# A two-layer diffusion backbone on one core: layer 0's gate stage with TensorE in the program's order, column sums two steps behind their squares, one adaLN row block for each gate tile

## The chip, the cores and the metric

The kernel runs on one core of one Trainium2 chip. The metric is the device time of one execution in microseconds (us), taken as the median of several runs; lower is better.

The engines are named as in the profile: PE is TensorE (matrix products into PSUM), PEld its weight loads, DVE is VectorE, ACT is ScalarE, POOL is GpSimd, SP is SyncE, which issues most DMAs. Each engine works through its own instruction stream in order and waits on semaphores for the others.

## The reference, cut to what matters

Two post-norm layers over 1024 latent tokens with 256 context tokens ahead of them share one weight set per layer: layer 0 is multi-head latent attention, layer 1 differential attention. All of it is float32.

```
m = silu(c) @ ada_w[i] + ada_b[i]            # adaLN: shift, scale, gate, for c and for c_ctx
h = x * (1 + scale) + shift                   # and h_c from ctx in the same way
q_lat, kv_lat, k_pe, gate = split(h @ w_in)   # 256 + 128 + 32 + 1024 columns
q = rms_norm(q_lat, g_qa) @ w_qb              # 16 heads of 64 + 32
kv = rms_norm(kv_lat, g_kva) @ w_kvb          # 16 heads of 64 + 64
k_pe, q_pe = rope(k_pe), rope(q_pe)
o = softmax(q k^T * scale) v
x = layer_norm(ALPHA * x + gate_ada * ((o * silu(gate)) @ out_w), ln_g, ln_b)
```

The stage at issue is the one that computes `silu(gate)` for all 1280 tokens. Beside it the kernel prepares the up-projection weights of layer 0 and does the adaLN sums that are needed later: shift and scale of layer 1 and the gate of layer 0.

## The kernel before, in words

Matrix products are done in pieces: every float32 operand is split into a high and a low part, and `mm3` (L185 to L187) issues three matmuls for each product. The first stretch computes h and its split, then the latent columns of `w_in` for ten tiles of 128 tokens (`lat_post` transposes the result and writes the rope keys to the DRAM buffer `kp_d`).

The gate stage (`p0g`) then runs over four column blocks q of 256 columns and ten token tiles each. One `gate_tile` is 24 matmuls of 128x256 into a PSUM bank of tag `a` or `d`, two of each, a SiLU on ACT (tile `gg`) and a DMA to `sg_d`. `gate_w` loads and splits the next block's weights: eight loads `wgs`, a cast on ACT (`wgH`) and a subtraction on POOL (`wgL`). The two weight buffers take turns, so block q+2 can be split only when block q has been used.

Beside the tiles runs the generator `beside_gates`, from which two steps are taken for each tile. It has two parts:

- `up_weights` loads `w_qb` in four pieces of 128x768 and the key half of `w_kv` in two of 128x512, scales each on DVE, casts it on ACT and forms the low part on POOL; applies rope to the keys in three chunks of tokens (`kr`); and bounds the column norms of the V, K and Q weights. For that ACT squares 512 columns into `wsq`, PE sums the columns with a matrix of ones (`onr`) into a bank of tag `c`, of which there are two, and DVE takes the maximum into `vm` (L415). With the largest rope key, broadcast by one matmul (L438), these give the power-of-two scales `vsc0`, `ksc0`, `qsc0`. Last it writes the split rope keys to `kpf_d`.
- `ada_dve` goes through three thirds of `ada_w`: shift and scale of layer 1, gate of layer 0. For each of eight row blocks of 512 KB (`adw`, three buffers) DVE adds it, times one scalar per row, into two accumulators (L467, L469), one for c and one for c_ctx, one buffer each. At the end of a third PE sums over partitions: 8 matmuls of one column per accumulator for shift and scale (L476), 4 matmuls of 512 columns for the gate (L488).

After the stage `ab1_of` and `h1_range` bound layer 1's input (two matmuls, L507, and some twenty small DVE instructions), and layer 0's first head follows: `prod_k`, `prod_q` and `prod_v0` with three PSUM pairs of tag `a`.

What sets the order: most of the program is issued in the order of a scheduler that works at build time with its own estimates, engine by engine. In a `manual_schedule` block PE instead keeps the order in which the program issues its instructions; `man.close()` ends such a block. Before, PE is under the scheduler from the end of the latent products to the end of the gate stage. The instruction streams are fixed at build time either way.

Of the kernel before, what the change touches and what calls it, by code (L numbers as in the profile page):

```python
# [9 lines left out]
F32 = mybir.dt.float32  # L10
# [43 lines left out]
def hybrid_kernel(  # L54
# [317 lines left out]
    def up_weights(pa):  # L372

        for j in range(2):
            for hh in range(2):
                c = slice(hh * 768, hh * 768 + 768)
                ws = pa.tile([P, 768], F32, tag="ws2", bufs=1, name=nm("ws2"))
                sp.dma_start(ws, w_qb[j * P:(j + 1) * P, c])
                dve.tensor_scalar_mul(ws, ws, gqa[:, j:j + 1])
                split(wqH[:, j, c], wqL[:, j, c], ws, e_lo=pool)  # L380
                yield
        for hh in range(2):
            c = slice(hh * 512, hh * 512 + 512)
            kv_weight(c, wkH[:, c], wkL[:, c], rot(pa, [P, 512], F32, "wkv"))
            yield

        kr = pa.tile([ROPE, NTOK], F32, name="kr")
        for c0, n in CHUNKS:
            c = slice(c0, c0 + n)
            kt = pa.tile([ROPE, 512], F32, tag="kt", name=nm("kt"))  # L390
            sp.dma_start(kt[:, :n], kp_d[:, c])
            if c0 < SEQ:
                tabs = []
                for j in range(2):
                    tb = pa.tile([ROPE, 512], F32, tag=f"ktab{j}", name=nm("ktab"))
                    sp.dma_start(tb, cs0[j, :ROPE, c])
                    tabs.append(tb)
                rope(kt, n, tabs[0], tabs[1], rot(pa, [ROPE, 512], F32, "rsw"), kr[:, c])
            else:
                dve.tensor_copy(kr[:, c], kt[:, :n])  # L400
            yield


        vm = pa.tile([P, 8], F32, name="vm")

        def col_norms(dst, parts, n):
            wsq = pa.tile([P, 2, 512], F32R, tag="wsq", name=nm("wsq"))
            for c0 in range(0, n, 512):
                for j, f in enumerate(parts):
                    f(wsq[:, j, :], slice(c0, c0 + 512))  # L410
                yield
                bk = bank("c")
                for j, f in enumerate(parts):
                    pe.matmul(bk, onr, wsq[:, j, :], start=j == 0, stop=j == len(parts) - 1)
                dve.tensor_reduce(vm[:, 6:7], bk, axis=AX.X, op=ALU.max)  # L415
                if c0:
                    dve.tensor_tensor(dst, dst, vm[:, 6:7], op=ALU.max)
                else:
                    dve.tensor_copy(dst, vm[:, 6:7])
                yield  # L420

        def sq_v(dst, c):
            wv = pa.tile([P, 512], F32, tag="wvq", bufs=1, name=nm("wvq"))
            sp.dma_start(wv, w_kv[:, 1024 + c.start:1024 + c.stop])
            act.activation(dst, wv, AF.Square, scale=gkva)

        yield from col_norms(vm[:, 0:1], [sq_v], 1024)
        yield from col_norms(vm[:, 1:2], [lambda d_, c: act.activation(d_, fv(wkH[:, c]), AF.Square)], 1024)
        yield from col_norms(vm[:, 2:3], [lambda d_, c, j=j: act.activation(d_, fv(wqH[:, j, c]), AF.Square)
                                          for j in range(2)], 1536)  # L430
# [4 lines left out]
        dve.tensor_reduce(vm[:ROPE, 3:4], kr, axis=AX.X, op=ALU.max, apply_absolute_value=True)  # L435
# [11 lines left out]
        kh_ = pa.tile([P, 768], F32, tag="ws2", bufs=1, name=nm("ws2")).bitcast(F16)[:ROPE, :NTOK]  # L447
        kl_ = pa.tile([P, 2, 512], F32R, tag="wsq", name=nm("wsq")).rearrange(
            "p a b -> p (a b)").bitcast(F16)[:ROPE, :NTOK]
# [5 lines left out]
    man.close()  # L455

    def ada_dve(tile_, bk_, thirds):

        for layer, g in thirds:
            acc = [tile_(f"acc{s}") for s in range(2)]  # L460
            for k in range(KT):
                w = tile_("adw")
                sp.dma_start(w, ada_w[layer, k * P:(k + 1) * P, g * D:(g + 1) * D])
                for s, a_ in enumerate(acc):
                    ck = sc[:, 2 * k + s:2 * k + s + 1]
                    if k == 0:
                        dve.tensor_scalar_mul(a_, w, ck)  # L467
                    else:
                        dve.scalar_tensor_tensor(a_, w, ck, a_, op0=ALU.mult, op1=ALU.add)  # L469
                yield  # L470
            yield
            if g < 2:
                cb = bk_()
# [8 lines left out]
                continue  # L482
            gr = tile_("adw")[:1, :]
            sp.dma_start(gr, ada_b[layer:layer + 1, g * D:(g + 1) * D])
            for s, a_ in enumerate(acc):
                for c0 in (0, 512):
                    bk = bk_()
# [3 lines left out]
                yield  # L491

# [7 lines left out]
    def h1_range(bk):  # L500

        for i in range(2):
            dve.tensor_reduce(hm[:, i:i + 1], ab1[:, i, :, :].rearrange("p a b -> p (a b)"), axis=AX.X, op=ALU.max,
                              apply_absolute_value=True)
# [975 lines left out]
```

## Time and profile before

| | us |
|---|---|
| median of 3 runs | 1860.38 |
| the runs | 1852.12, 1860.38, 1868.84 |
| span of the profiled execution | 1870.0 |
| gate stage, first tile behind the latent products to the last | 99.7 to 250.0 |
| first score of layer 0 | 284.2 |

The profiled execution is given by its span, from the first to the last instruction; it lies 1.2 us above the slowest of the runs shown, and no time of its own is listed beside it. In the profile, "idle" is the time in which an engine had nothing to run, and the name behind the arrow is the instruction whose end let it go on. A matmul's row shows its latency; neighbouring matmuls overlap, so the time of a tile is read from start to start. The granted clock is the share of full TensorE speed in a stretch.

### The profile page before, as it was taken

How to read it: one execution, taken by the hardware profiler on the slowest of the kernel's cores; microseconds unless marked ns; L12 is line 12 of the kernel's file. 1: busy time of each engine (PE TensorE's matmuls, PEld its weight loads, DVE VectorE, ACT ScalarE, POOL GpSimd, SP SyncE). 2: the span in 40 equal slices, each digit the busy share in tenths (PEclk: the TensorE clock that was granted, in tenths of full speed). 3: DMA queues.
4: the chain of work that ended last, by engine and by line, in shares of the span. 5: the costliest groups of instructions: out<-in, count | busy, mean ns of one | idle time of the engine just before them, and what ended most of it. 6: DMA issues, size and time to landing. Idle time of an engine off the chain costs nothing. (4 is left out here: it accounts for less than half of the span.)

```text
span 1870.0 us, 36547 instructions
## 1 busy us (share of the span) xinstructions
PE 1696.2 (91%) x14468; PEld 1237.0 (66%) x14468; DVE 1245.6 (67%) x2072; ACT 1077.1 (58%) x2143; POOL 835.2 (45%) x741
## 2 busy tenths in 40 slices
PE   7889998999999998868979999999999999988998
PEld 3888965656666565556756576767666666666776
DVE  7546766565565657526764777787877777878674
ACT  3432047867777787711123667676767676767542
POOL 1443026767767676646662213222222222433654
PEclk9999799999999999979999999999999999999999
DMA  8245630111111113043333222222121212224341
GB/s 307 62 126 182 189 108 18 39 33 36 42 44 32 32 41 100 25 164 123 124 127 106 71 63 66 62 64 58 56 49 44 59 46 61 63 53 139 99 131 68
DMA packets 111225, 154.84 MB, mean 83 GB/s; under 512 B 13415, under 2 KB 84679, under 8 KB 111054
## 3 DMA queue, kind: packets, MB, share of 16 engines
q1 hardware_dynamic: 104238, 146.22, 26.1%
q10 hardware_dynamic: 6816, 6.29, 1.0%
q8 instruction: 114, 1.87, 0.4%
q14 instruction: 57, 0.47, 0.1%
HBM read 98.65 MB, written 27.07 MB: 67 GB/s over the span
## 5 line engine op out<-in xcount | busy, mean ns | idle before, releaser
L716 POOL TENSOR_TENSOR pl<-p,ph 128x1024 f16<-128x1024 f32 (+1 forms) x176 | 362.8, 2066 | 155.9 <-ACT ph L715 129.5
L1167 ACT ACTIVATE p<-ps_b,mx 128x512 f32<-128x512 f32 (+1 forms) x384 | 230.6, 618 | 83.1 <-DVE mx L1163 82.7
L696 DVE TENSOR_REDUCE mx<-ps_a 128x1 f32<-128x1024 f32 x128 | 155.6, 1223 | 138.2 <-PE ps_a L694 138.2
L714 ACT ACTIVATE p<-ps_a,esc 128x1024 f32<-128x1024 f32 (+1 forms) x176 | 189.2, 1075 | 100.4 <-PE ps_a L772 94.5
L715 ACT CAST ph<-p 128x1024 f16<-128x1024 f32 (+1 forms) x176 | 177.1, 1006 | 5.5
L1161 DVE TENSOR_REDUCE mx<-ps_b 128x1 f32<-128x512 f32 x256 | 165.6, 682 | 0.0
L785 PE MATMUL ps_d<-Vh,pl 128*128 128x65 f16 x1344 | 147.5, 195 | 5.2 <-POOL pl L716 5.1
L782 PE MATMUL ps_d<-Vh,ph 128*128 128x65 f16 x1344 | 149.5, 196 | 0.0
L784 PE MATMUL ps_d<-Vl,ph 128*128 128x64 f16 x1344 | 148.3, 193 | 0.0
L185 PE MATMUL ps_b<-h1H,wH 128*128 128x512 f16 (+1 forms) x384 | 133.5, 348 | 14.1 <-DVE pl L182 6.7
L185 PE MATMUL ps_b<-wH,h1H 128*128 128x256 f16 x512 | 139.5, 272 | 4.4 <-ACT p L1167 4.2
L1192 POOL TENSOR_TENSOR sm<-sm,us 128x1 f32<-128x1 f32 x64 | 18.3, 285 | 271.9 <-DVE sm L1171 258.6
L187 PE MATMUL ps_b<-wH,h1L 128*128 128x256 f16 x512 | 139.5, 273 | 0.0
L186 PE MATMUL ps_b<-wL,h1H 128*128 128x256 f16 x512 | 139.5, 272 | 0.0
L1144 PE MATMUL ps_b<-KS,QS 128*128 128x512 f16 (+1 forms) x384 | 126.1, 345 | 12.0 <-DVE pl L182 6.1
L782 PEld LDWEIGHTS <-ph 128*128 128x128 f16 x1344 | 124.2, 98 | 18.4 <-issue 5.5
L187 PE MATMUL ps_b<-h1H,wL 128*128 128x512 f16 (+1 forms) x384 | 133.2, 347 | 0.8 <-DVE wL L182 0.8
L186 PE MATMUL ps_b<-h1L,wH 128*128 128x512 f16 (+1 forms) x384 | 133.4, 347 | 0.0
L784 PEld LDWEIGHTS <-ph 128*128 128x128 f16 x1344 | 124.9, 99 | 12.4 <-issue 0.8
L770 PE MATMUL ps_a<-qH,KH 100*128 100x512 f16 x320 | 123.6, 386 | 9.7 <-ACT p L714 4.3
L1145 PE MATMUL ps_b<-KS,Q 128*128 128x512 f16 (+1 forms) x384 | 129.1, 345 | 0.0
L785 PEld LDWEIGHTS <-pl 128*128 128x128 f16 x1344 | 124.1, 98 | 6.6 <-POOL pl L716 6.5
(370 smaller groups left out, 5161.9 us busy)
## 6 DMA issues: line engine op xcount, KB each, us to landing
ws<-in_dw SPq DMA_DIRECT2D x30, 512.0 KB, 3.8
adw<-in_ada_w SPq DMA_DIRECT2D x24, 512.0 KB, 5.0
g<-sg_d SPq DMA_DIRECT2D x18, 512.0 KB, 3.7
adaw<-in_ada_w SPq DMA_DIRECT2D x16, 512.0 KB, 7.1
sg_d<-gg ACTq DMA_DIRECT2D x40, 128.0 KB, 2.8
o<-o_d SPq DMA_DIRECT2D x10, 512.0 KB, 3.5
o_d<-op SPq DMA_DIRECT2D x7, 640.0 KB, 3.7
xt<-in_xT SPq DMA_DIRECT2D x16, 256.0 KB, 3.6
```

The lines of the kernel that those rows point to most:

```text
L185: pe.matmul(ps, aH, bH, start=start, stop=False, skip_group_check=skip)
L186: pe.matmul(ps, aH, bL, start=False, stop=False, skip_group_check=skip)
L187: pe.matmul(ps, aL, bH, start=False, stop=stop, skip_group_check=skip)
L696: dve.tensor_reduce(mx[:, t, 0:1], ps, axis=AX.X, op=ALU.max)
L714: act.activation(p32[:, :n], st, AF.Exp, scale=esc0)
L715: act.copy(ph[:, :n], p32[:, :n])
L716: pool.tensor_tensor(pl[:, :n], p32[:, :n], ph[:, :n], op=ALU.subtract)
L782: pe.matmul(pv[:, t, :], ph[:, ts], Vh[:, k, h, :], start=(k == kcs[0] and t == 0), stop=False, skip_group_check=True)
L784: pe.matmul(pv[:, t, :V0], ph[:, ts], Vl[:, k, h, :], start=False, stop=False, skip_group_check=True)
L785: pe.matmul(pv[:, t, :], pl[:, ts], Vh[:, k, h, :], start=False, stop=(k == NT - 1), skip_group_check=True)
L1161: dve.tensor_reduce(mx[:, 2 + 2 * m + i:3 + 2 * m + i], b, axis=AX.X, op=ALU.max, negate=True)
L1167: act.activation(p[m][:, c0:c0 + n], b, AF.Exp, bias=nb, accum_out=sm[:, 2 + 3 * m + i:3 + 3 * m + i])
```

## The change

Four things change, all in the gate stage.

1. PE stays in the program's order from the latent products through the gate stage into layer 0: the `man.close()` behind `up_weights` and the second `enter_context` are gone.
2. `up_weights` is cut into jobs that share four rotating buffers `u`. The squares of V come first, then the weights, then rope chunks between the squares of K, then the squares of Q. `column_sums` for a square is issued when two more squares have been issued behind it (`len(wait) == 3`), with three buffers `wsq` instead of one pair. Two of five of its steps end a gate tile's share.
3. One step of the side generator is taken for each tile instead of two. In `ada_dve` a step is one row block; there are three accumulator buffers instead of two single ones, and the column groups of a third (`finish`) are issued during the first two blocks of the next.
4. `ab1_of` moves to the start of head 0's first step and `h1_range` becomes a generator that runs beside it, with a PSUM pair in place of a `c` bank.

```diff
-    man.close()
+        norms = ((0, [sq_v], 1024), (1, [lambda d_, c: act.activation(d_, fv(wkH[:, c]), AF.Square)], 1024),
+                 (2, [lambda d_, c, j=j: act.activation(d_, fv(wqH[:, j, c]), AF.Square) for j in range(2)], 1536))
...
+        def column_sums(sq, i, c0, first, stop):
+            if first:
+                cur[0] = bank("c")
+            pe.matmul(cur[0], onr, sq, start=first, stop=stop)
+            if stop:
+                dst = vm[:, i:i + 1]
+                d_ = vm[:, 6:7] if c0 else dst
+                dve.tensor_reduce(d_, cur[0], axis=AX.X, op=ALU.max)
...
+        def square(f, i, c0, first, stop):
+            sq = pa.tile([P, 512], F32R, tag="wsq", bufs=3, name=nm("wsq"))
+            f(sq, slice(c0, c0 + 512))
+            wait.append((sq, i, c0, first, stop))
+            if len(wait) == 3:
+                column_sums(*wait.pop(0))
+        sq = [(square, a) for a in jobs]
+        rc = [(rope_chunk, a) for a in CHUNKS]
+        for f, a in (sq[:2] + [(q_weight, (j, hh)) for j in range(2) for hh in range(2)] + [(k_weight, (hh,)) for hh in range(2)]
+                     + [rc[0], sq[2], rc[1], sq[3], rc[2]] + sq[4:]):
+            f(*a)
             yield
...
+        end = iter(())
+        for layer, g in thirds:
+            acc = []
+            for k in range(KT):
+                w = tile_("adw")
+                sp.dma_start(w, ada_w[layer, k * P:(k + 1) * P, g * D:(g + 1) * D])
+                for s in range(2):
+                    ck = sc[:, 2 * k + s:2 * k + s + 1]
+                    if k == 0:
+                        acc.append(tile_("acc"))
+                        dve.tensor_scalar_mul(acc[s], w, ck)
+                        if s == 0:
+                            next(end, None)
+                    else:
+                        dve.scalar_tensor_tensor(acc[s], w, ck, acc[s], op0=ALU.mult, op1=ALU.add)
+                if k:
+                    next(end, None)
+                yield
+            end = finish(layer, g, acc)
...
-                for _ in range(2):
-                    next(side, None)
+                next(side, None)
...
-    ab1_of()
-    h1_range(bank("c"))
     p0.close()
-    man.enter_context(tc.manual_schedule(engines={ENG[c] for c in MAN}))
...
+            if h == 0:
+                ab1_of()
+            hr = [(h1_range(pair), (0, 1, 0, 1, 1))] if h == 0 else []
```

The change moves instructions on every engine. Three places:

On DVE beside the first column sums. Before, rope (`kr`) is nearly through when the first maximum (L415, of bank `ps_c_1233`) comes, and no rope stands between the maxima:

```order
L400 COPY kr<-kt_1193 32x256
L435 TENSOR_REDUCE vm<-kr 32x1
L415 TENSOR_REDUCE vm<-ps_c_1233 128x1
L419 COPY vm<-vm 128x1
L379 TENSOR_SCALAR ws_150_1059<-ws_150_1059,gqa 128x768
L415 TENSOR_REDUCE vm<-ps_c_1272 128x1
L417 TENSOR_TENSOR vm<-vm 128x1
L415 TENSOR_REDUCE vm<-ps_c_1310 128x1
```

Now the maxima (L407) stand between the instructions of rope, whose inputs and scratch tile are buffers `u`:

```order
L291 TENSOR_SCALAR u_1142<-u_1142,gkva 128x512
L407 TENSOR_REDUCE vm<-ps_c_1160 128x1
L277 STREAM_SHUFFLE u_1153<-u_1147 32x512
L278 TENSOR_TENSOR kr<-u_1147,u_1149 32x512
L407 TENSOR_REDUCE vm<-ps_c_1208 128x1
L279 TENSOR_TENSOR u_1153<-u_1153,u_1150 32x512
L409 TENSOR_TENSOR vm<-vm 128x1
L280 TENSOR_TENSOR kr<-kr,u_1153 32x512
L277 STREAM_SHUFFLE u_1201<-u_1195 32x512
L407 TENSOR_REDUCE vm<-ps_c_1249 128x1
```

The maximum of the second bank (`ps_c_1208`) moved behind the shuffle and the product of the first rope chunk; the fourth column sum on PE writes that bank again, right after the third and two gate tiles after the second.

On PE at the first adaLN column group. Before, it stands in the middle of a gate tile (`ps_a_1901`), nine and a half tiles after L438, and nine matmuls later the second group follows:

```order
L185 MATMUL ps_a_1901<-wgH_1315,hH 128x256
L186 MATMUL ps_a_1901<-wgL_1316,hH 128x256
L187 MATMUL ps_a_1901<-wgH_1315,hL 128x256
L476 MATMUL ps_c_1723<-ones,acc_211_1533 128x1 x8
L185 MATMUL ps_a_1901<-wgH_1315,hH 128x256
```

Now it stands between two tiles, eight tiles after L448, and the second group follows after the whole tile `ps_a_1743`:

```order
L185 MATMUL ps_d_1698<-wgH_974,hH 128x256
L186 MATMUL ps_d_1698<-wgL_975,hH 128x256
L187 MATMUL ps_d_1698<-wgH_974,hL 128x256
L470 MATMUL ps_c_1730<-ones,acc_1442 128x1 x8
L185 MATMUL ps_a_1743<-wgH_1341,hH 128x256
```

The group comes a tile and a half earlier after the end of the weight chain, and the two groups of a third are further apart.

On DVE at the start of layer 0. Before, h1_range's last instruction (`hic`), the scaled V weights (`p`) and the low part of the keys (`stkL`) come ahead of the rope shuffle of the queries:

```order
L516 TENSOR_SCALAR hic<-kci 128x1
L291 TENSOR_SCALAR p_335_2506<-p_335_2506,gkva 128x512
L182 SCALAR_TENSOR_TENSOR stkL_2494<-ps_a_2524,ksc_69,stkH_2493 128x1024
L291 TENSOR_SCALAR p_335_2506<-p_335_2506,gkva 128x512
L182 SCALAR_TENSOR_TENSOR stkL_2494<-ps_a_2533,ksc_69,stkH_2493 128x256
L277 STREAM_SHUFFLE rsw_2491<-ps_a_2541 128x1024
L278 TENSOR_TENSOR rr_2492<-ps_a_2541,cosA 128x1024
```

Now the shuffle is the first of the stage:

```order
L483 TENSOR_TENSOR acc_2045<-adw_2340,ps_c_2380 1x512
L277 STREAM_SHUFFLE rsw_2465<-ps_a_2515 128x1024
L291 TENSOR_SCALAR p_341_2480<-p_341_2480,gkva 128x512 x2
L182 SCALAR_TENSOR_TENSOR stkL_2468<-ps_a_2498,ksc_69,stkH_2467 128x1024
L182 SCALAR_TENSOR_TENSOR stkL_2468<-ps_a_2507,ksc_69,stkH_2467 128x256
L278 TENSOR_TENSOR rr_2466<-ps_a_2515,cosA 128x1024
```

The shuffle moved ahead of the V weights and `stkL`, and h1_range's instructions are gone from here.

More of the change, by code (lines that the diff above doesn't have):

```diff
@@ L372, in up_weights @@
     def up_weights(pa):
[L374 to L382, printed above, removed]
-            c = slice(hh * 512, hh * 512 + 512)
-            kv_weight(c, wkH[:, c], wkL[:, c], rot(pa, [P, 512], F32, "wkv"))
-            yield
@@ L399, in up_weights @@
             else:
                 dve.tensor_copy(kr[:, c], kt[:, :n])
-            yield
[L404 to L430, printed above, removed]
+        wait = []
@@ L453, in up_weights, with ada_dve, finish @@
         yield
-    man.close()
[L457 to L471, printed above, removed]
+    def ada_dve(tile_, thirds):
+        def finish(layer, g, acc):
             if g < 2:
-                cb = bk_()
+                cb = bank("c")
                 for s, a_ in enumerate(acc):
```

67 lines of the change are left out of this document (48 added, 19 removed).

## The prediction

> **What bounds the kernel now.** I read the page first, then the stretches of time around the change, then what TensorE (PE) waits for in them. PE is the busiest engine of the program:
>
> ```profile
> PE 1696.2 (91%) x14468; PEld 1237.0 (66%) x14468; DVE 1245.6 (67%) x2072; ACT 1077.1 (58%) x2143; POOL 835.2 (45%) x741
> ```
>
> What the change moves lies between the gate tile that starts at 114.17 us and the first score of layer 0 at 284.24. Before and after that the engines keep their order, so only this stretch is priced. Its parts (columns: stretch, length, busy time and count of PE, PEld, DVE, ACT, POOL, granted clock, DMA share, GB/s), then all of PE's long waits in it, the starts of two neighbouring gate tiles, and one column sum with the tile behind it:
>
> ```profile
> 114.17:152.42 38.25, 31.41 (x228) 30.29 (x226) 16.67 (x35) 14.49 (x32) 15.12 (x17) 0.91 0.39 113
> 180.37:199.00 18.63, 14.11 (x69) 14.11 (x69) 12.14 (x13) 0.39 (x1) 1.00 (x1) 0.64 0.53 155
> 212.77:222.94 10.17, 10.17 (x64) 10.17 (x63) 5.20 (x7) 0.38 (x1) 0.00 (x0) 0.67 0.42 132
> 250.03:284.24 34.21, 27.41 (x125) 19.48 (x123) 26.99 (x40) 23.44 (x26) 14.11 (x9) 1.00 0.32 90
> 250.67:252.82 2.15, 2.15 (x12) 1.79 (x11) 1.98 (x15) 1.75 (x4) 1.59 (x2) 1.00 0.44 143
> 252.82:262.55 9.73, 9.11 (x39) 6.84 (x38) 9.09 (x12) 6.26 (x9) 2.57 (x2) 1.00 0.23 58
> ...
> PE ps_c L476 <- DVE acc L469: 4.5, 1, 4.5
> PE ps_c L414 <- ACT wsq L428: 4.1, 1, 4.1
> PE ps_c L414 <- ACT wsq L425: 2.8, 1, 2.8
> ...
> 102.64 0.28 PE L185 MATMUL ps_a<-wgH,hH 128*128 128x256 f32 x1
> 105.53 0.28 PE L185 MATMUL ps_d<-wgH,hH 128*128 128x256 f32 x1
> ...
> 119.92 0.39 PE L414 MATMUL ps_c<-wsq,onr 128*128 128x512 f32 x1
> 120.15 0.28 PE L185 MATMUL ps_a<-wgH,hH 128*128 128x256 f32 x1
> ```
>
> A gate tile takes 105.53 - 102.64 = 2.88 us (0.12 for each of 24 matmuls), a column sum 0.23. So PE is the bound through the gates, but for 11.4 us of waits, and it loses more than these: the granted clock is 0.91, 0.64 and 0.67 where the waits and the L476 groups lie. In the first stretch nine tiles (25.9) and ten sums (2.3) should take 28.2 of its 38.25 us. The other 10.0 are 6.9 of waits and 3.1 of slow clock: **one us of waiting costs 1.45**.
>
> **Part A: weights and column sums.** Their chain ends with the matmul L438 at 152.42; its successor L448 stands three gate tiles earlier. The squares of V are made first now, so both old L414 waits go. A new one comes: two PSUM banks serve the column sums, and on DVE the maximum that frees the second bank for the fourth sum stands behind the first rope shuffle. That shuffle writes a `u` buffer which must first be released by the last key-weight split on POOL. Behind PE's waiting matmul all further gate tiles queue. The rows for it:
>
> ```profile
> 109.01 0.62 DVE L379 TENSOR_SCALAR ws<-ws,gqa 128x768 f32<-128x768 f32 x1 [7.34 <-DMA ws<-in_w_qb]
> 110.57 1.85 POOL L177 TENSOR_TENSOR wqL<-ws,wqH 128x768 fp32r<-128x768 f32 x1 [5.73 <-ACT wqH L176]
> ...
> 105.00:110.00 5.00, 5.00 (x44) 5.00 (x43) 0.62 (x1) 0.72 (x2) 0.00 (x0) 1.00 0.89 267
> ...
> L177 POOL TENSOR_TENSOR wqL<-ws,wqH 128x768 fp32r<-128x768 f32 x4 | 7.3, 1834 | 18.2 <-ACT wqH L176 18.2
> L177 POOL TENSOR_TENSOR wkL<-wkv,wkH 128x512 fp32r<-128x512 f32 x2 | 3.3, 1655 | 2.0 <-ACT wkH L176 2.0
> ...
> L415 DVE TENSOR_REDUCE vm<-ps_c 128x1 f32<-128x512 f32 x7 | 4.8, 687 | 12.4 <-PE ps_c L414 12.4
> L277 DVE STREAM_SHUFFLE rsw<-kt 32x512 f32<-32x512 f32 x2 | 1.5, 742 | 0.0
> L278 DVE TENSOR_TENSOR kr<-kt,ktab 32x512 f32<-32x512 f32 x2 | 1.3, 658 | 0.0
> ...
> ws<-in_w_qb SPq DMA_DIRECT2D x4, 384.0 KB, 5.3
> ```
>
> On SP the two V loads (512 KB) now go ahead of the first query weight: at 267 GB/s 2.0 us, so POOL starts at 110.57 + 2.0 = 112.5. Its six splits take 7.3 + 3.3, until 123.1. Shuffle, product and maximum (0.74 + 0.66 + 0.69) end at 125.2. PE is there after two tiles and three sums, at 114.17 + 6.45 = 120.6. It waits 4.6 us, with its slow clock 6.7. The new part A is six tiles (17.3), ten sums (2.3) and 6.7: 26.3. The old one less three tiles is 38.25 - 8.64 = 29.6. **A: -3.3.** From below: if the V loads cost nothing POOL starts at 110.57, the maximum ends at 123.3, the wait is 2.7 and A is -6.1. From above: the last key weight is issued only when the second query split gives its buffer back, at 112.5 + 3.7 = 116.2. With a landing of 5.3 (the `ws` row), 1.6 from arrival to POOL (109.01 to 110.57), its split and 2.1 the maximum ends at 126.9; A is -0.9. I take the middle, which rests on the most rows.
>
> The later sums and L448 find their squares and maxima done by the same rows, if each rope load lands within a tile or two; that is rival 3. The squares themselves are ACT's, which is busy 14.5 of the 38.25 us, and hide beside the tiles.
>
> **Part B: adaLN and its column groups.** Rows of DVE and PE:
>
> ```profile
> 152.42 0.40 PE L438 MATMUL ps_c<-idr,vm 32*128 32x32 f32 x2
> ...
> 161.17 1.42 DVE L467 TENSOR_SCALAR acc<-adw,sc 128x1024 f32<-128x1024 f32 x2 [4.32 <-DMA adw<-in_ada_w]
> 165.34 20.69 DVE L469 SCALAR_TENSOR_TENSOR acc<-adw,sc,acc 128x1024 f32<-128x1024 f32 x14 [2.76 <-DMA adw<-in_ada_w]
> 194.03 12.05 DVE L469 SCALAR_TENSOR_TENSOR acc<-adw,sc,acc 128x1024 f32<-128x1024 f32 x10
> ...
> 184.89 3.01 PE L476 MATMUL ps_c<-ones,acc 128*128 128x1 f32 x16 [4.52 <-DVE acc L469]
> 189.83 3.41 PE L476 MATMUL ps_c<-ones,acc 128*128 128x1 f32 x16
> 193.88 0.41 PE L185 MATMUL ps_d<-wgH,hH 128*128 128x256 f32 x1
> 199.00 0.37 PE L185 MATMUL ps_a<-wgH,hH 128*128 128x256 f32 x1
> 212.77 1.84 PE L476 MATMUL ps_c<-ones,acc 128*128 128x1 f32 x16
> ```
>
> The loads of adaLN still stand behind the end of the weight chain, so I count from L438. DVE's first long sum began 165.34 - 152.42 = 12.9 us after it. The first group needs 13 of them: at 12.05 / 10 = 1.2 us each, 12.9 + 15.7 = 28.6. PE now comes to it after eight tiles instead of nine and a half, at 0.3 + 23.0 = 23.4. The wait is 5.2 us at least, against 4.5. In the old order POOL's splits for the last gate weights ran beside these sums (20.69 / 14 = 1.48 each). Now their buffer comes free only with the eighth tile, so they meet the last four: 4 x 0.28 = 1.1. I take 6.3, that is +1.8; at 1.48 throughout it is 8.7, +4.2. The second and third group pairs have cover: PE needs over 30 us for eight tiles and two groups, DVE 1.4 + 14 x 1.48 = 22 for a third, with some 5 us held at the second group's result.
>
> The groups themselves: the first pair cost 18.63 less 36 matmuls at 0.12 (4.3) and the wait, 9.8 us; the second, which waited for nothing, 10.17 less 30 matmuls (3.6), 6.6. Each group now has a whole tile behind it, where nine matmuls lay between two. I keep 16.4 for the four, as the nearest rows have it, bounded by four times 1.84 = 7.4 (-9.0) and by four times a slow group with a slow tile, 3.41 + (199.00 - 193.88 - 2.88) = 5.65 each, 22.6 (+6.2). **B: +1.8.** The gates' last matmuls (L488, now L482) cost the same. `gates_d`, the V weights and the rope tables follow them on SP some 5 us before the gates end instead of 10. The product that reads the tables comes on DVE after the shuffle, the V-weight products and both stkL, some 9 us past that end, so this stays covered by about 14 us; without the cover it would cost what is missing of a load.
>
> **Part C: start of layer 0.** h1_range leaves the gap between the stages, with its matmuls of 0.36 us:
>
> ```profile
> 250.03 0.60 PE L507 MATMUL ps_c<-idr,hm 128*128 128x128 f32 x4
> 250.39 0.48 PE L185 MATMUL ps_a<-latH,wkH 128*128 128x512 f32 x1
> 255.28 0.50 PE L185 MATMUL ps_a<-latH,wqH 128*128 128x512 f32 x1
> 262.55 1.27 DVE L599 SCALAR_TENSOR_TENSOR Vl<-ps_a,vsc,Vh 128x1024 f16<-128x1024 f32 x1
> 284.24 0.39 PE L770 MATMUL ps_a<-qH,KH 100*128 100x512 f16 x1 [0.84 <-DVE qH L706]
> 300.24 1.23 DVE L696 TENSOR_REDUCE mx<-ps_a 128x1 f32<-128x1024 f32 x1 [1.98 <-PE ps_a L694]
> ```
>
> DVE is busy 27.0 of the 34.2 us there and sets the pace. Its first instruction is now the rope shuffle, which waits 255.28 - 250.39 = 4.9 us for its product; the V-weight products and both stkL, which stood ahead of it, queue behind, and PE's next product waits for the bank that stkL frees. Before, DVE began 2.8 us after the gates (252.82) and was through the rope at 262.55, 12.5 after them, with 9.1 us of work. Begun at 4.9, the same work ends at 14.0: +1.5. The price is no higher than the later start, 4.9 - 2.8 = 2.1, and may be nothing where DVE's later idle time takes it in; I take +1.2. The small DVE instructions of h1_range, 2.0 us busy in the row from 250.67, return inside the first head's step, ahead of the one (L723) that gives the next step its running maximum; the idle 1.98 us behind its old place take most of them in. I take +0.6 (0.4 to 2.6), less the 0.36 saved.
>
> **Sum.** -3.3 + 1.8 + 1.2 + 0.6 - 0.4 = -0.1 us: no change. The profiled span is 1870.0 us, so 1869.9; it lies 9.6 above the median of the runs shown (1860.4, from 1852.1 to 1868.8), and I give the time by the median: 1860.
>
> **Rivals.** (1) *The clock holds.* Each group is followed by a full tile, so PE never looks idle: the second pair costs 2 x 1.84 instead of 6.6, and of the first only the group behind the wait is slow, 3.0 + 2.2 + 1.84 = 7.1 instead of 9.8; with part A at its lower end the sum is -0.1 - 5.6 - 2.8, 1852. Against it: the clock was 0.67 from 212.77 on, where PE had not waited. The Trainium skill, page "TensorE: Matmul & The Clock Gate", section "What's actually happening", has the clock halved by an idle window of about 3.4 us and restored by a busy one; if only idleness counts, this rival holds, and the trace speaks against it with 0.67 without a wait. (2) *Slower: each group drops the clock by itself*, since the clock has come back over the tile between: +6.2 and the longer wait +2.4, 1869. It decides as soon as the tile behind each of four groups takes 5 us. For it: the tile 193.88 to 199.00. (3) *The rope chain serializes the sums*: the three later maxima each wait for a buffer, a load and DVE as the first does; at 4.6 x 1.45 twice more, 1873.
>
> **Chances.** Forecast 0.45, (1) 0.25, (2) 0.17, (3) 0.08, and 0.05 for a gain beyond (1), in which nearly all of the 11.4 us of waits and their slow clock go. About 1% (18.6 us) is what can be told from no change. Each case alone stays inside it but the last; on the slower side it is passed where (2) and (3) come together or either meets part C at its upper end, about a third of their 0.25. So faster 0.06, same 0.86, slower 0.08. The range reaches from (1) to (3) and by 4 to 5 us beyond, half the spread of the runs shown: 1846 to 1877.
>
> **What would show it.** Right: no wait on ACT squares, one wait of 3 to 7 us on DVE at the fourth column sum, one of 5 to 9 before the first adaLN group, slow clock behind both, the first score 35 us after the gates, and a gate stretch as long as before within 5 us. Wrong: the first adaLN group ready when PE comes, a granted clock near 1 around the groups, or waits at every column sum.

## The result, and the profile after

| | before | changed |
|---|---|---|
| median, us | 1864.87 (12 runs, 1852.12 to 1868.84) | 1864.66 (12 runs, 1861.00 to 1869.33) |
| ratio, 95% interval | | 1.0007 [0.9993, 1.0020] |
| profiled execution: own time, span | not listed, 1870.0 | 1863.27, 1861.5 |

The ratio is taken over the fast runs of both kernels and is not the quotient of the two medians. No change, as forecast. The parts of the sum came out otherwise, though, and the profile of before turned out to be a poor yardstick: its span alone is longer than each of the twelve times of that kernel in this table. The first line of the changed kernel's page (engine, busy time, share of the span, instructions):

```profile
PE 1688.1 (91%) x14468; PEld 1232.8 (66%) x14468; DVE 1239.5 (67%) x2069; ACT 1076.3 (58%) x2143; POOL 834.9 (45%) x741
```

PE is busy 8.1 us less with the same number of instructions, which points to the clock it was granted and not to its work. The changed kernel by stretches, from the start of the gate stage to head 0 (columns: stretch, length, busy time and count of PE, PEld, DVE, ACT, POOL, granted clock, DMA share, GB/s): first gate tile to first column sum, first sum to L448, L448 to the end of the last gate tile, that to the first score, first score to DVE's first head result.

```profile
97.45:115.60 18.15, 18.12 (x152) 17.78 (x150) 2.65 (x6) 8.04 (x24) 6.62 (x10) 1.00 0.63 179
115.60:143.69 28.09, 21.85 (x156) 20.82 (x154) 18.62 (x36) 13.30 (x28) 16.03 (x15) 0.88 0.36 103
143.69:244.50 100.81, 96.38 (x748) 92.75 (x747) 65.03 (x73) 15.25 (x38) 13.52 (x13) 0.95 0.61 181
244.50:281.06 36.56, 28.01 (x120) 20.07 (x119) 23.45 (x25) 23.10 (x26) 14.07 (x9) 0.95 0.36 108
281.06:305.55 24.49, 20.76 (x189) 11.75 (x190) 13.95 (x28) 14.34 (x14) 13.49 (x7) 0.86 0.03 9
```

The gate stage takes 18.15 + 28.09 + 100.81 = 147.05 us, 7 less than the 154.0 (96.03 to 250.03) of before's profile. Both are counted from the first gate tile; the 99.7 in the table of the profile before is the start of its second tile. Head 0's opening takes 24.49 where it took 19.60 (284.24 to 303.84). PE's waits of the changed kernel from the first gate tile to the first head result:

```profile
PE ps_c L470 <- DVE acc L501: 4.4, 1, 4.4
PE ps_a L185 <- DVE stkL L182: 3.4, 1, 3.4
PE ps_c L403 <- DVE vm L407: 3.2, 1, 3.2
PE ps_c L403 <- ACT wkH L176: 3.0, 1, 3.0
...
PE ps_a L787 <- DVE qH L723: 2.2, 2, 1.4
PE ps_a L722 <- DVE ng L719: 1.9, 1, 1.9
PE ps_a L722 <- DVE hm L284: 1.4, 1, 1.4
```

The old waits on squares are gone. Two waits stand at the column sums, one of them forecast; one before the adaLN groups; one on `stkL` at the start of layer 0; two new ones in head 0, listed under `hm` and `qH`. The rows of the column sums, from the timelines of POOL, SP, DVE, ACT and PE, in order of time:

```profile
115.89 8.05 POOL L177 TENSOR_TENSOR wqL<-u,wqH 128x768 fp32r<-128x768 f32 x4 [9.30 <-ACT wqH L176]
117.77 2.46 SPq L290 DMA_DIRECT2D u<-in_w_kv  x2
122.97 0.63 ACT L394 ACTIVATE wsq<-wkH 128x512 fp32r<-128x512 f32 x1
123.25 0.98 DVE L291 TENSOR_SCALAR u<-u,gkva 128x512 f32<-128x512 f32 x1 [0.96 <-DMA u<-in_w_kv]
123.91 2.67 POOL L177 TENSOR_TENSOR wkL<-u,wkH 128x512 fp32r<-128x512 f32 x2
124.15 0.68 DVE L407 TENSOR_REDUCE vm<-ps_c 128x1 f32<-128x512 f32 x1
124.27 0.62 ACT L176 CAST wkH<-u 128x512 fp32r<-128x512 f32 x1 [0.40 <-DVE u L291]
124.98 0.47 PE L403 MATMUL ps_c<-wsq,onr 128*128 128x512 f32 x1 [3.03 <-ACT wkH L176]
126.63 0.71 DVE L277 STREAM_SHUFFLE u<-u 32x512 f32<-32x512 f32 x1
127.25 0.66 DVE L278 TENSOR_TENSOR kr<-u,u 32x512 f32<-32x512 f32 x1
127.84 0.67 DVE L407 TENSOR_REDUCE vm<-ps_c 128x1 f32<-128x512 f32 x1
128.66 0.77 PE L403 MATMUL ps_c<-wsq,onr 128*128 128x512 f32 x1 [3.21 <-DVE vm L407]
```

The fourth sum (128.66) waits along the chain of part A: POOL's last key split ends at 126.58, the shuffle, the product and the maximum follow, and PE goes on. The third sum (124.98) waits too, which the middle value did not hold. The profile names ACT's cast at 124.27, but that cast is of the other half of the key weights; the square that the sum reads is done at 122.97 + 0.63 = 123.60, and in after_again 3.2 us before its sum starts. What the third sum also needs is the bank of the first one. The maximum that frees it ends at 124.15 + 0.68 = 124.83, 0.15 us before the sum, as the second maximum ends 0.15 before the fourth sum, and the distance is 0.14 or 0.15 in all nine profiles with the new column sums. On DVE this first maximum stands behind the scaling of the second key weight (123.25), which waited for its load: the key weights are only loaded from 117.77 on, when query splits have given their `u` buffers back.

### The profile page after: what moved, and what is told of

Its sections match the earlier page's. It is cut to its first block, busy times and chain, and to the rows that moved or that the text cites. A ratio compares the mean times of both kernels' runs of the same rounds, so it can differ in the third digit from the quotient of the medians.

```text
span 1861.5 us, 36543 instructions
## 1 busy us (share of the span) xinstructions
PE 1688.1 (91%) x14468; PEld 1232.8 (66%) x14468; DVE 1239.5 (67%) x2069; ACT 1076.3 (58%) x2143; POOL 834.9 (45%) x741
## 5 line engine op out<-in xcount | busy, mean ns | idle before, releaser
L802 PE MATMUL ps_d<-Vh,pl 128*128 128x65 f16 x1344 | 147.0, 194 | 6.7 <-POOL pl L733 6.7
L185 PE MATMUL ps_b<-h1H,wH 128*128 128x512 f16 (+1 forms) x384 | 133.5, 348 | 14.1 <-DVE pl L182 7.1
```

The costliest lines, as they stand in the source:

```text
L185: pe.matmul(ps, aH, bH, start=start, stop=False, skip_group_check=skip)
L802: pe.matmul(pv[:, t, :], pl[:, ts], Vh[:, k, h, :], start=False, stop=(k == NT - 1), skip_group_check=True)
```

## Experiments

Each is timed or profiled beside the kernel before. "Gate start to head" is the time from the first gate tile to DVE's first head result; all parts of the change lie in it. The letters (R and N, W and G, and so on) are those of the two rival expectations in the quoted text of each experiment.

**range_back: the fourth part undone.** `ab1_of` and `h1_range` go back to the end of the gate stage.

```diff
+    ab1_of()
+    for _ in h1_range(lambda: bank("c")):
+        pass
     p0.close()
...
-            if h == 0:
-                ab1_of()
-            hr = [(h1_range(pair), (0, 1, 0, 1, 1))] if h == 0 else []
-            run_step(units0(h, 0), hr + [(max0(h, 1), (1, 1, 2, 1, 1)), (max0(h, 2), (0, 1, 0, 1)),
+            run_step(units0(h, 0), [(max0(h, 1), (1, 1, 2, 1, 1)), (max0(h, 2), (0, 1, 0, 1)),
```

> The changed kernel with ab1_of and h1_range put back at the end of the gate stage. Theory R (the gate stage won 7.0 us and the move of h1_range gave them back: 2.3 at the start of layer 0, where DVE now begins with the rope shuffle, and 4.9 in head 0's first step): from the last gate tile to the first score 34.2 us as before the change instead of 36.6, from there to DVE's first head result 19.6 instead of 24.5, and a ratio to the kernel before of 0.9962 (1857.5 us). Rival N (the shorter gate stage is no real gain, it is made up elsewhere or was chance of one execution): the ratio stays within 0.9985 to 1.002.

Measured: ratio 1.0005 [0.9995, 1.0016], so N by the total. In place it was R: end of gates to first score 34.89, first score to head result 19.61, the first head result at 300.20 instead of 305.55. These contradict each other, and a second execution, range_back_again below, comes back to it.

**range_moved: the fourth part alone**, on the kernel before (the diff above reversed, with `h1_range` made a generator).

> The kernel before with the move of h1_range alone. Theory R: slower by 2.3 + 4.9 us, ratio 1.0039 (1.003 to 1.0045), with PE's wait for stkL at the start of layer 0 and two waits for hm and qH in the first step. Rival N: the move costs what I forecast, 1.2 + 0.6 - 0.4 us, ratio 1.0008.

Measured: ratio 1.0033 [1.0019, 1.0046], as R has it; first score to head result 24.57, with the waits on `stkL` (3.4), `hm` (1.4) and `qH` (2.2 in all). The 2.3 us that R adds at the start of layer 0 are not clear: end of gates to first score is 35.18, and 34.21 to 36.50 in three executions of before. Its gate stage, which is that of before, took 146.2 us, not 154.0: the first hint that the profile of before was a slow one there.

**group_late: two more tiles ahead of the first adaLN groups.**

```diff
             end = finish(layer, g, acc)
+            if (layer, g) == thirds[0]:
+                yield
+                yield
         yield
```

> The changed kernel with two gate tiles more ahead of the first adaLN column groups. Theory W (only PE's waits drop the clock; a group with a whole tile behind it costs 1.8 us): the wait of 4.4 us goes, the first pair costs 3.5 us like the second instead of 7.8, granted clock 1.00 there; 8.7 us off, ratio to the kernel before 0.996. Rival G (a first group is slow by itself, or the later group makes DVE's next third late): the wait goes, but 3 us or more of the 8.7 stay, ratio 0.9977 or above.

Measured: ratio 0.9976 [0.9967, 0.9985], a little faster than the kernel before and the changed one. The wait of 4.4 us is gone, all four groups take 1.84 us, and the clock behind L448 is 1.00 to the end of the gates. Gate start to head is 198.22, 9.9 less than the 208.10 of the changed kernel, for a wait of 4.4: the slow clock behind it went too. In place this is W; the total lies between W's 0.996 and G's 0.9977, so some 3 us of the gain do not show in it.

**groups_together: the second third's two groups back to back.**

```diff
                                   start=True, stop=True)
-                    yield
+                    if g == 0:
+                        yield
                 dve.tensor_tensor(cols1
```

> The changed kernel with both column groups of the second third back to back between the same two tiles (the pair that waits for nothing). Theory L (what drops the clock is a stretch of single-column matmuls longer than one group, not a wait alone): granted clock near 0.7 behind them, the pair costs 6 to 7 us instead of 3.5, ratio to the kernel before 1.002. Rival W (only waits drop the clock): the pair costs 3.5 to 3.7 us at clock 1.00, ratio 1.0007 as for the change itself.

Measured: ratio 1.0042 [1.0024, 1.0061], so L, and by more than its 1.002. The profile is of the slowest of the seven executions, 10 us above their median. The stretch around the pair, in which PE is never idle but the granted clock is 0.80, and the pair itself in the timeline (32 matmuls in one row, 4.76 us instead of 2 x 1.84):

```profile
195.00:212.00 17.00, 17.00 (x121) 17.00 (x120) 11.27 (x20) 1.54 (x4) 0.00 (x0) 0.80 0.54 167
```

```profile
200.79 4.76 PE L470 MATMUL ps_c<-ones,acc 128*128 128x1 f32 x32
```

The gate tile behind the pair starts at 205.41 and the next one at 210.32, 4.91 us for 2.88. So the pair costs 210.32 - 200.79 - 2.88 = 6.7 us, in L's range.

**before_again, after_again and a third before: the same kernels profiled again.**

> The kernel before once more, unchanged, for a second profiled execution. Theory V (its stages vary from one execution to the next): the gate stage, from its first tile to the end of its last, takes 145 to 150 us instead of the 154.0 of the first profile, as it did with the same gate instructions in range_moved (146.2); the wait of the second column sum on the ACT square (4.1) is under 3 us and the granted clock at 212 to 223 us is 0.9 or more; and the stretch from 740 to 765 us, which ran at a clock of 0.56 to 0.76 in the first profile, may run at 1.00, 7.7 us shorter. Rival F (the times are the kernel's own): the gate stage is 153 to 155 again, both waits on squares are back, and 740 to 765 us is slow again.

> The changed kernel once more, unchanged, for a second profiled execution. Theory V2 (the new order is steadier): the gate stage takes 146 to 149 us (147.0 in the first profile) with the same three waits, 2.5 to 3.5 at the third sum on ACT, 2.5 to 3.5 at the fourth on DVE and 4 to 5 before the first adaLN group; from the first score to DVE's first head result 24 to 25 us; 740 to 765 us at clock 1.00. Rival F2 (it varies as the old one does): the gate stage differs by 4 us or more from the first profile, or one of the three waits is gone, or the stretch behind 740 us is slow.

> The kernel before a third time, for its gate stage. Theory V (the 154.0 us of the first profile are the rarer case): gate stage 145 to 150 us, second pair of adaLN groups at 1.84 us each with the clock at 0.95 or more around them, waits on squares 3 to 5 us in all. Rival F (the stage takes 154 about as often as 147): 152 to 156 us, waits on squares over 6 us, or slow clock around the second pair.

The stretches by execution, us (the last row of the changed kernel is from after_timed, below):

| | gate start to first sum | to L438 / L448 | to end of gates | to first score | to head result | sum |
|---|---|---|---|---|---|---|
| before, first | 23.89 | 32.50 | 97.61 | 34.21 | 19.60 | 207.81 |
| before_again | 23.91 | 29.22 | 93.83 | 35.59 | 19.60 | 202.15 |
| before, third | 23.89 | 29.25 | 94.28 | 36.50 | 20.86 | 204.78 |
| changed, first | 18.15 | 28.09 | 100.81 | 36.56 | 24.49 | 208.10 |
| after_again | 18.14 | 27.67 | 100.63 | 36.55 | 24.47 | 207.46 |
| after_timed | 18.14 | 27.75 | 100.97 | 37.73 | 24.41 | 209.00 |

The stretch behind L438 in the first profile of before, in before_again, and the second pair of groups in the timeline of before_again:

```profile
152.42:250.03 97.61, 93.09 (x675) 89.47 (x675) 64.95 (x73) 13.71 (x34) 14.32 (x9) 0.90 0.60 186
```

```profile
151.61:245.44 93.83, 89.70 (x676) 86.03 (x676) 65.17 (x73) 13.69 (x34) 13.53 (x9) 0.93 0.65 193
```

```profile
210.90 1.84 PE L476 MATMUL ps_c<-ones,acc 128*128 128x1 f32 x16
213.76 1.84 PE L476 MATMUL ps_c<-ones,acc 128*128 128x1 f32 x16
```

Their single times were 1862.12 and 1865.32 (before) and 1864.46 (changed). The old gate stage takes 147.0 and 147.4 in these two of before (V). The second sum's wait on its square is 3.2 and 3.1 where it was 2.8, the third sum's 0.5 and 0.6 where it was 4.1 (V's text gives the 4.1 to the second), and the clock is 1.00 around the second pair of groups. The changed kernel repeats its waits and its 146.4 to 147.05 (V2). The first profile of before was slow in just the two places from which the prediction priced A and B.

It was also slow once more where the change does nothing. From 740 to 770 us, before and then the changed kernel:

```profile
740.00:770.00 30.00, 25.25 (x237) 13.97 (x235) 20.52 (x22) 20.89 (x20) 17.06 (x8) 0.77 0.26 79
```

```profile
740.00:770.00 30.00, 26.63 (x347) 16.70 (x343) 20.59 (x27) 25.99 (x26) 23.26 (x12) 1.00 0.30 87
```

Between the same two head results before needs 764.62 - 742.95 = 21.67 us there, the changed kernel 758.63 - 744.70 = 13.93: 7.7 us of slow clock. before_again, range_back and range_moved ran this stretch at 1.00, groups_together at 0.77 too, order_only at 0.83.

**after_timed and range_back_again: both timed on one chip.**

> The changed kernel once more, timed on the same chip as the next two. Theory W (the change loses some 6 us in head 0 and at the start of layer 0, and gains nothing in the gate stage against two of three executions of before; slow-clock stretches behind 740 us, which differ from execution to execution, hide part of it): ratio 1.000 to 1.0035, first head result 24 to 25 us behind the first score, gate stage 146 to 148.5 us. Rival X (the gate stage of before is the slow one, 154 us, in most executions, so that its loss and the gain cancel): ratio 0.9985 to 1.0005.

> range_back once more: the changed kernel with h1_range back at the end of the gate stage. Its first head result came 5 us earlier than the changed kernel's, and its total no earlier. Theory Y (the missing gain is the spread of late slow-clock stretches over executions): this time the ratio to the kernel before is 0.9965 to 0.9990 and lies 0.001 to 0.0035 below that of the changed kernel beside it; the profile may or may not show the clock below 0.95 at 870 to 910 us. Rival Z (the gain is given back each time at the end of layer 0): the ratio is within 0.001 of the changed kernel's again, with a clock of 0.91 at 870 to 910 us and a step of 4 to 6 us there.

Measured: 1.0008 [0.9992, 1.0024] and 0.9974 [0.9961, 0.9987]. The first lies in W's range and just above X's, whose 1.0005 the interval includes; the gate stage of before, 147 in two further executions, speaks for W. For the second Y holds: 0.0034 below the changed kernel. Why the first range_back showed none of it in its total stays open. Set beside the changed kernel's first profile, its DVE rows are 5.4 us ahead until some 740 us, 7.6 at 867 and only 2.1 at 887, at the end of layer 0. But after_again and after_timed lose 5.5 and 5.6 us against that same profile between the same two rows, so the step is a quick stretch of that one execution, with a granted clock of 1.00 from 870 to 890 us where range_back, after_again and after_timed have 0.91, and not something that range_back gives back. range_back_again is 9.6 us ahead at the first head result and 6.6 at the end.

**order_only: the first part alone**, TensorE in program order, all else as before.

```diff
-    man.close()
-
     def ada_dve(tile_, bk_, thirds):
...
     p0.close()
-    man.enter_context(tc.manual_schedule(engines={ENG[c] for c in MAN}))
```

> The kernel before with the first of the four parts alone: TensorE in the program's order through the gate stage. The column sums stay where they are; the first pair of adaLN groups, which the scheduler had put nine and a half tiles behind L438, now stands five tiles behind it (14.4 us), the second pair six tiles on, the gate's four matmuls five tiles on instead of eleven. Theory S (PE waits for DVE's sums, 28.6 us behind L438 for the first third, some 22 us for each next one): waits of about 13 before the first group, 3 to 8 before the second and before the last, with slow clock behind them 20 to 30 us in all, less the 4.5 of before: gate stage 163 to 180 us, ratio 1.007 to 1.015. Rival T (DVE's sums are themselves held back by loads that follow PE's progress, or the clock holds): gate stage 150 to 160, ratio 1.000 to 1.005.

Measured: ratio 1.0068 [1.0035, 1.0100], gate stage 162.6. Both lie a touch below S's ranges (from 1.007 and 163), far from T's 150 to 160. PE's waits in the stage:

```profile
PE ps_c L474 <- DVE acc L467: 16.9, 2, 16.1
PE ps_c L414 <- ACT wsq L425: 2.9, 1, 2.9
PE ps_c L486 <- DVE acc L467: 2.5, 1, 2.5
```

The 16.1 us stand before the first group, where S had about 13; the waits before the second pair (0.75) and before the last sums (2.5) fall short of its 3 to 8. So the program's order alone costs 0.7%. Parts two and three pay it back together; neither was tried alone, so how much each pays is open.

**back_late: range_back and group_late together.**

> The changed kernel with both mends: h1_range and ab1_of back at the end of the gate stage, and two more tiles ahead of the first adaLN groups. Theory K (each mend wins in its place; that range_back showed none in its total is the spread of later stages): the first head result comes 10 to 13 us earlier behind the first gate tile than in the changed kernel (208.1), 195 to 198 us, and the ratio to the kernel before is 0.993 to 0.997. Rival G (what is won in head 0 is given back before the end): the first head result as early as that, but the ratio 0.9970 to 0.9990, no better than group_late's 0.9976.

Measured: ratio 0.9959 [0.9938, 0.9979], gate start to head 296.26 - 99.41 = 196.85: K, though the interval reaches into G's range. The two mends do not simply add up. The gate stage takes 136.75 us, but the start of layer 0 39.23 (the window from the end of the gates to the first score), where range_back and range_back_again had 34.89 and 33.77:

```profile
236.16:275.39 39.23, 30.73 (x129) 21.14 (x127) 28.81 (x42) 23.44 (x26) 15.23 (x10) 0.95 0.42 116
```

`h1_range` is back ahead of layer 0 here, and yet the scheduler has put the rope shuffle ahead of the V weights and `stkL` on DVE again, and PE waits 3.0 us for `stkL`. So that wait belongs to the order on DVE and not to the place of `h1_range` alone. keys_first has the same order and 39.11; the cause of the rest was not pursued.

**keys_first: back_late, and the key weights and their squares ahead.**

```diff
-        for f, a in (sq[:2] + [(q_weight, (j, hh)) for j in range(2) for hh in range(2)] + [(k_weight, (hh,)) for hh in range(2)]
-                     + [rc[0], sq[2], rc[1], sq[3], rc[2]] + sq[4:]):
+        for f, a in (sq[:2] + [(k_weight, (hh,)) for hh in range(2)] + [(q_weight, (j, hh)) for j in range(2) for hh in range(2)]
+                     + [sq[2], sq[3], rc[0], sq[4], rc[1], sq[5], rc[2]] + sq[6:]):
```

> back_late with the key weights ahead of the query weights and their squares right behind, so that the third and fourth column sums wait neither for a late key weight nor for a maximum behind the rope shuffle. Theory A2 (part A's two waits, 3.0 on ACT and 3.2 on DVE with their slow clock, cost 6 to 9 us): the wait on wkH is gone, one wait of 0 to 3 us is left at the fifth sum (DVE's maximum behind the shuffle, whose buffer POOL's last query split releases), the stretch from the first column sum to L448 takes 21 to 25 us instead of 28.4, the gate stage 128 to 133 instead of 136.7, ratio to before 0.991 to 0.9945. Rival B2 (POOL's six splits end no earlier, and PE only meets them at a later sum): the waits move to the fifth and sixth sums with the same 5 to 7 us, the stretch takes 27 to 30 us, ratio 0.995 to 0.997.

Measured: ratio 0.9934 [0.9913, 0.9955], the fastest of all; its runs were 1847.31 to 1852.11. Gate start to head is 192.96. The total lies in A2's range; the gate stage, 134.49, is above its 128 to 133, and the stretch from the first sum to L448 lies between A2 and B2: 143.28 - 117.11 = 26.17 us, where A2 had 21 to 25, B2 27 to 30 and back_late 28.4. The name `wkH` is gone from PE's waits, but the third sum still waits, for the same first maximum:

```profile
120.44 3.28 DVE L382 TENSOR_SCALAR u<-u,gqa 128x768 f32<-128x768 f32 x2 [1.47 <-DMA u<-in_w_qb]
123.64 1.27 DVE L407 TENSOR_REDUCE vm<-ps_c 128x1 f32<-128x512 f32 x2
124.47 0.77 PE L403 MATMUL ps_c<-wsq,onr 128*128 128x512 f32 x1 [3.87 <-DVE vm L407]
```

That maximum now stands on DVE behind the scaling of all four query weights, where it stood behind that of the second key weight, and PE waits 3.87 us for the bank that it frees. With 0.93 at a later sum 4.8 us of the 6.2 to 6.6 are still there. Putting the maxima ahead of the scaling was not tried.

How far the local times carry, against the mean of the three executions of before, 204.9 us, with 1 us as 0.00054 of the total:

| | gate start to head | ratio from it | measured |
|---|---|---|---|
| changed (mean of three) | 208.2 | 1.0018 | 1.0007, 1.0008 |
| range_back, range_back_again | 202.26, 198.97 | 0.9986, 0.9968 | 1.0005, 0.9974 |
| range_moved | 205.92 | 1.0005 | 1.0033 |
| group_late | 198.22 | 0.9964 | 0.9976 |
| groups_together | 212.24 | 1.0039 | 1.0042 |
| order_only | 215.92 | 1.0059 | 1.0068 |
| back_late | 196.85 | 0.9957 | 0.9959 |
| keys_first | 192.96 | 0.9936 | 0.9934 |

All but the first range_back and range_moved agree within 0.0012. Each local time but the first row's is of one execution, and the three of before spread over 5.7 us (0.003), so more than a rough agreement is not to be had. What the two miss is 3.5 and 5 us, less than the 7.7 of the slow stretch above; that such stretches are the reason is not shown.

## Why the prediction was right, and where it was wrong

**The total** was right, but in good part by luck: none of the four parts came out as forecast. The sum of -0.1 us was made against one execution of before, and that execution was 3 to 6 us longer from gate start to head than the next two. Against it the changed kernel's first profile gives 208.10 - 207.81 = +0.3, because B came 7.2 us cheaper than forecast and A, C and D together 7.6 dearer. Three executions against three it is 208.2 - 204.9 = +3.3, for which the two intervals around 1.0007 and 1.0008 leave room.

**Part A: -3.3 forecast.** Measured, with one tile of 2.88 less in the stretch, 28.09 - (32.50 - 2.88) = -1.5 against the first profile, inside the bounds of -6.1 and -0.9; against the two others +1.75 and +1.72. The step "the squares of V are made first now, so both old L414 waits go" held, and the shuffle chain behind POOL's last key split is there, with 3.2 us instead of 4.6. The step that failed is "A new one comes": there are two. The third sum waits 3.0 us for the first bank, whose maximum stands behind the scaling of the late second key weight (the order on DVE ahead of the prediction has that L291 right before it), and the prediction looked at the second bank alone. The late load was only in its upper bound. And the 6.9 us that were to be won are 3.7 in other executions.

**Part B: +1.8 forecast.** Measured, with three tiles of 2.88 more in the stretch, 100.81 - (97.61 + 8.64) = -5.4, and -1.7 and -2.1 against the other two. The wait of 6.3 is 4.4, since DVE's first long sum begins 154.87 - 143.69 = 11.2 us after L448 and not 12.9; the 13 sums take the forecast 15.7 + 1.1 = 16.8. The step that failed is "I keep 16.4 for the four". DVE's sums and the groups of the changed kernel:

```profile
154.87 16.83 DVE L501 SCALAR_TENSOR_TENSOR acc<-adw,sc,acc 128x1024 f32<-128x1024 f32 x13 [1.14 <-DMA adw<-in_ada_w]
171.76 3.57 PE L470 MATMUL ps_c<-ones,acc 128*128 128x1 f32 x16 [4.43 <-DVE acc L501]
180.46 1.85 PE L470 MATMUL ps_c<-ones,acc 128*128 128x1 f32 x16
202.41 1.84 PE L470 MATMUL ps_c<-ones,acc 128*128 128x1 f32 x16
```

The first group with its tile takes 180.46 - 171.76 - 2.88 = 5.8 us more than a tile, the third 207.07 - 202.41 - 2.88 = 1.8, so the four cost some 11 us and not 16.4. Only the group behind the wait and the tile after it are slow, which is rival 1's mechanism. Its time of 1852 did not come, since A stayed at -1.5 where that rival had -6.1, and C and D took the rest. What spoke against it, the clock of 0.67 without a wait, did not come again around that pair in the three other executions with the old groups. Rival 2 is out: no tile behind a group other than the first took 5 us.

**Part C: +1.2 forecast**, with L507's 0.36 off. Measured 36.56 - 34.21 = +2.35; three against three 36.9 - 35.4 = +1.5. The shuffle comes first and PE's product waits 3.4 for `stkL`, as said. The price itself is not clear of the spread: range_moved, with the same wait, took 35.18, and the three executions of before 34.21 to 36.50.

**Part D: +0.6 forecast, 0.4 to 2.6.** Measured 24.49 - 19.60 = +4.9, and 24.41 to 25.43 in every execution with h1_range in head 0, far outside the bounds. The step that failed is "the idle 1.98 us behind its old place take most of them in". DVE and POOL of the changed kernel:

```profile
292.42 0.48 DVE L723 SCALAR_TENSOR_TENSOR qcH<-ps_a,sh,selt 2x256 f16<-2x256 f32 x1
292.55 2.12 POOL L733 TENSOR_TENSOR pl<-p,ph 128x1024 f16<-128x1024 f32 x1 [0.82 <-ACT ph L732]
292.93 1.76 DVE L529 TENSOR_TENSOR hm<-hm 128x1 f32<-128x1 f32 x1
294.61 0.15 DVE L530 SCALAR_TENSOR_TENSOR hm<-hm 128x1 f32<-128x1 f32 x1
294.68 0.15 DVE L719 TENSOR_REDUCE ng<-mx 128x4 fp32r<-128x8 f32 x1
...
296.16 0.74 DVE L723 SCALAR_TENSOR_TENSOR qH<-ps_a,sh,selt 4x512 f16<-4x512 f32 x1
```

L529, one element per partition, took 0.16 us as L511 in its old place (0.16 in range_back too) and takes 1.76 here: it ends at 294.69, POOL's subtraction at 294.67. PE's product for the next maximum (L722) reads `ng` (L719), which stands behind it on DVE, and starts late. Twelve more instructions of h1_range go ahead of `qH`, and the scores that wait for `qH` begin 296.96 - 281.06 = 15.9 us behind the first score. In before's profile they began 298.31 - 284.24 = 14.1 behind it. Of the 4.9 us 1.8 are that; the rest comes behind it, with slow clock (the window from 295 to 300 us, and rows of PE's timeline):

```profile
295.00:300.00 5.00, 3.62 (x21) 1.56 (x22) 1.80 (x11) 0.69 (x2) 2.12 (x1) 0.65 0.08 20
```

```profile
294.98 0.22 PE L722 MATMUL ps_a<-idr,ng 128*4 128x128 f32 x1 [1.44 <-DVE hm L284]
296.96 0.58 PE L787 MATMUL ps_a<-qH,KH 100*128 100x512 f16 x1 [1.38 <-DVE qH L723]
297.33 0.63 PE L788 MATMUL ps_a<-qH,KL 96*128 96x512 f16 x1
```

The score matmuls take 0.63 instead of 0.38 us there. That range_back and range_back_again return to 19.6 us and range_moved alone gives 24.57 shows the move as the cause. That L529's length comes from POOL rests on the ends of the two rows, which agree within 0.03 us in all six profiles with h1_range there, and on L533: it has two inputs too, runs at 295.31 between two of POOL's subtractions, and takes 0.16.

**What would show it**: the wait at the fourth sum (3.2) and the slow clock behind both waits came as said; the wait before the first group fell short of its 5 to 9 and the first score came at 36.6 instead of 35. The gate stretch was 7 us shorter than in the first profile, and within 1 us of the two others. Rival 3 is out: the third and the fourth sum waited for a maximum, and no later one did.

## What to carry to other kernels

One profile of a kernel before is one draw: price a gain from a wait or a slow clock in it only after asking whether another execution shows it too, since here 7 us of the gate stage and 7.7 us elsewhere were gone in the next. Work that is small where nothing else runs is not small in the middle of a tight loop: it is priced by who queues behind it on its engine and by what the other engines do at that moment, not by its busy time. And the waits that are left in front of PE cost more than they last, so that shifting one consumer by two tiles won 0.3% on top of a re-ordering that had won nothing. Last, the name that a profile puts behind a wait is inferred: ask what the waiting instruction reads and which bank it writes, since the cast that was named for the third sum had nothing to do with it, and the run that did away with it met the same wait again.

## What the runs showed of the hardware

- A vector instruction with two inputs in SBUF did not end before POOL's subtraction: L529 ended with it in all six profiles, 1.76 us for one element per partition, against 0.16 alone. The Trainium skill, page "SBUF — State Buffer", section "Who interferes with whom", has this: a VectorE instruction with two SBUF inputs and a GpSimd instruction that reads SBUF share a port pair, and the one that starts second waits for the end of the first. The trace agrees; POOL had started 0.38 us earlier.
- The granted clock fell without any idle of PE: 0.67 around the old second pair in the first profile, 0.80 from 195 to 212 us in groups_together. Groups of 16 one-column matmuls kept the clock in the second pair of every profile that has a whole tile between the two; with nine matmuls between them they kept it in three of four (before, before_again, the third before and range_moved), with none they lost it in the one profile there is. More than this tendency the runs don't show.
- The same program takes slow-clock stretches in different places in different executions (740 to 770 us at 0.77 or 1.00). The Trainium skill, page "TensorE: Matmul & The Clock Gate", section "What's actually happening", has a window that runs freely and not with the kernel, so that the outcome depends on where in it the work falls. That fits these differences; no run here moves the window itself.
